# A hybrid attention layer in fp32 on one core: stationary operands of 64 rows become operands of 128 rows

## The chip, the cores and the metric

One of the eight cores of a Trainium2 chip runs the kernel. The metric is the device time of one execution in microseconds (us), from the first to the last instruction. TensorE multiplies matrices, VectorE (DVE), ScalarE (ACT) and GpSimd (POOL) work elementwise, and SyncE (SP) issues most of the DMAs. Before a TensorE matmul its stationary operand has to be loaded into the array by an instruction of its own, LDWEIGHTS, which the profile lists as an engine PEld. The matmul then streams the moving operand through the array. A stationary operand of 128 rows by 128 columns fills the array; its rows are the axis that is summed over.

## The reference, cut to what matters

One layer of a decoder on 1024 tokens of width 1024, all in fp32. Three attentions run side by side on projections of the same normalised input; their gated sum is projected, and an MLP with a hidden width of 4096 follows. The edits touch the first attention (4 heads with two score maps each) and the compressed part of the third (8 heads in 2 groups, 63 compressed keys and values per group).

```python
# first attention: q, k [token, head, c, 64], v [token, head, 128]
s = jnp.einsum('bqhcd,bkhcd->cbhqk', qi, k).astype(jnp.float32) * scale + bias
p = jax.nn.softmax(jnp.where(mask, s, NEG_INF), axis=-1)
w = p[0] - lam * p[1]
return jnp.einsum('bhqk,bkhe->bqhe', w.astype(v.dtype), v)
...
# third attention, compressed part: kc, vc [block, group, 64]
s = jnp.einsum('bsgrd,bcgd->bgrsc', qg, kc).astype(jnp.float32) * scale
p_cmp = jnp.where(cmask, jax.nn.softmax(jnp.where(cmask, s, NEG_INF), axis=-1), 0.0)
o_cmp = jnp.einsum('bgrsc,bcgd->bsgrd', p_cmp.astype(vc.dtype), vc).reshape(B, S, H, D)
```

## The kernel before

**Numbers in two parts.** An fp32 value x is held as a high part (x rounded to the fp32r type that TensorE reads) and a low part x - high. `split` makes both: ScalarE copies the high part (L90), VectorE or GpSimd subtracts for the low part (L91). A dense product then takes three matmuls in `mm3`, high*high, high*low and low*high, at lines L118 to L120.

**Stages.** The program runs: normalisation and transposes of x while the first head's projection is made (the pool `p0` holds the buffers of that), the vectors of the relative position bias (`bias_vectors`), the compressor of the third attention's keys and values (pool `cp`), the first attention (stage A, `items_a`, four heads), the second (`items_b`), the third (stage C, `items_c`, two groups of four heads), then the merge of the branches and the MLP. TensorE's program order is the order in which the code is written; the order on the other engines comes from a scheduler. In the attentions `mix` weaves two streams into TensorE's order: the fine one (logits, transposes of probabilities, value products) and a dense one (the next head's projection in `project`, or the gates), by paces written in the code.

**Stage A.** For each head `project` computes 8 token tiles of q, k, v (384 columns). `vec` in `project_a` normalises them and lays q and k out in `tm`, 128 columns a block, and `to_state` turns the blocks over by TensorE transposes (L552), in groups of up to four, and copies each group to the state tile `st` (four blocks at a time on VectorE, L558, the fifth alone on ScalarE, L556). For map c the q block holds the high and the low part of q on 128 rows (64 each). The block `2 + c` of the state holds the high part of k twice, on both halves of the rows. The fifth block holds the low parts of k once for both maps: c = 0 on rows 0 to 63, c = 1 on rows 64 to 127. `logits` (L705) makes a score map of 64 to 512 columns in PSUM from two matmuls, with q as the stationary operand:

```python
n["logits"].append([(st[:, c * S:c * S + S], st[:, (2 + c) * S:(3 + c) * S]),
                    (st[half, c * S:c * S + S], st[half, 4 * S:5 * S])])
```

The first is a stationary operand of 128 rows (high and low q, against high k), the second one of 64 rows (high q alone, against low k). Between the row steps of an item stand projection matmuls with operands of 128 rows. VectorE finds each row's minimum (L719 and L729), ScalarE takes the exponential (L737) into `p` and so frees the logits' buffer (three buffers, `sc`), TensorE transposes `p` (L753), the result is split into `ph` and `pl`, and the value products follow two steps later.

**Stage C.** Each item (a head and 256 queries, 32 in all) begins with the compressed part: the logits of 64 compressed keys, masked, their exponentials `pc` (128 queries x 64), two transposes of `pc` into a tile of 64 rows, its split, and two value products with `vct` as the stationary operand (L895 with the high part of the probabilities, L896 with the low part). `vct` has 64 rows, the compressed blocks, and 128 columns, the high and the low part of the values. It writes the accumulator `ac`, of which there is one buffer, freed when the last item's output has been read (L902).

**Queues around it.** The loads of weights, of x and of the bias vectors' inputs (`rb`, `oh`, `mk`, lines L370 to L374) go through SP's queue, where an instruction that waits holds all behind it. The matmuls of `bias_vectors` (L378) stand between the first head's projection and the compressor's projection, whose weights are the eight loads of `wk`.

Of the kernel before, what the change touches and what calls it, by code (L numbers as in the profile page):

```python
# [11 lines left out]
F32 = mybir.dt.float32  # L12
# [5 lines left out]
P = 128  # L18
# [57 lines left out]
class Kernel:  # L76
# [97 lines left out]
    def run(self):  # L174
# [24 lines left out]
        self.st_n, self.tm_n = 7 * S, 768  # L199
# [7 lines left out]
        with tc.tile_pool(name="p0", side="right", **kw) as p0:  # L207
# [36 lines left out]
            self.bias_vectors(p0)  # L244
        with tc.tile_pool(name="cp", side="right", **kw) as cp:

            w1 = self.states[0].tile([P, 7, 4, 256], F32, name="w1", tag="st", bufs=1)
            for i in range(7):
                nc.sync.dma_start(w1[:, i], a["w1"][i // 4, :, (i % 4) * 4:(i % 4) * 4 + 4, :])
            z = self.compress_inputs(cp)  # L250
            self.spread_bias(0)
            self.mm = mm2
            self.mix(self.compress(cp, z, w1), self.gates(GATES[0]), PACE[5])
# [30 lines left out]
        nc.sync.dma_start(self.cmask, a["c_cmask"])  # L284
        for g in range(2):
# [41 lines left out]
    def constants(self, tmp):  # L327
# [36 lines left out]
        self.vct = c.tile([64, 2, P], F32R, name="vct")  # L364

    def bias_vectors(self, pool):
# [8 lines left out]
        bv = pool.tile([20, 2, 384], F32, name="bv")  # L375
        for i in range(2):
            ps = self.mm()
            nc.tensor.matmul(ps[0:20, 0:384], rb, oh[:, i, :], start=True, stop=True)  # L378
            nc.vector.tensor_tensor(bv[:, i, :], ps[0:20, 0:384], mk[:, i, :], op=ALU.add)
        self.bs = self.dram.tile([20, 2, 384], F32, name="bs")  # L380
        nc.sync.dma_start(self.bs, bv)
# [39 lines left out]
    def compress(self, cp, z, w1):  # L421
# [37 lines left out]
        for kv in range(2):  # L459
# [22 lines left out]
            else:  # L482
# [3 lines left out]
                self.split(self.vct[:, :, 0:64], self.vct[:, :, 64:128], vr)  # L486
# [81 lines left out]
    def project_a(self, h):  # L568
# [4 lines left out]
        n = dict(st=st, v=st[:, 5 * S:7 * S].rearrange("p (t x e) -> p t x e", x=2, e=P), logits=[])  # L573
        for c in range(2):
            half = slice(64 * c, 64 * c + 64)
            n["logits"].append([(st[:, c * S:c * S + S], st[:, (2 + c) * S:(3 + c) * S]),
                                (st[half, c * S:c * S + S], st[half, 4 * S:5 * S])])
        gain = self.gk[:, 0:1, :].to_broadcast([P, 2, HD])

        def vec(t, raw):  # L580
# [8 lines left out]
            kl = tm[:, 512:640].rearrange("p (c d) -> p c d", d=HD)  # L589
            nc.vector.tensor_tensor(kl, y[:, 2:4, :], kd[:, :, 0, :].bitcast(F32), op=ALU.subtract)  # L590
            return tm

        return self.project(self.a["wa"][h], 384, vec, (st, [i * S for i in range(5)])), n
# [364 lines left out]
    def items_c(self, g, sta):  # L958
        nc, at = self.nc, self.at
        bias4 = self.bias  # L960
        for r in range(4):
            for qb in range(4):
# [104 lines left out]
                def pv_c(blk=blk, hv=hv):  # L1067
                    ph, pl = blk["p"]
                    return hv(self.vct[:, g, :], ph[0:64, 0:256], pl[0:64, 0:256], True, False)
# [15 lines left out]
    def compressed(self, mem, ps, t):  # L1085

        nc = self.nc
        p = mem["c"] = self.at.tile([P, 64], F32, name="pc", tag="pc", bufs=4)
        m, l = mem["m"], mem["l"]
        nc.vector.tensor_tensor_reduce(ps, ps, self.cmask[:, t, :], 1.0, 3e38, ALU.add, ALU.min, m[:, 0, 0:1])  # L1090
        self.expo(p, ps, m[:, 0, 0:1], l[:, 0, 0:1])
# [490 lines left out]
```

## Time and profile before

| what | value |
|---|---|
| median of 3 executions | 2076.6 us (2073.64 to 2076.71) |
| span of the profiled execution | 2073.6 us |
| mean granted TensorE clock | 0.983 of full speed |
| TensorE matmuls | 1950.6 us busy (94%), 9806 instructions |
| TensorE weight loads | 1615.6 us (78%) |
| VectorE | 1420.5 us (69%) |
| ScalarE | 1019.3 us (49%) |
| GpSimd | 948.4 us (46%) |
| DMA | 219.47 MB, mean 106 GB/s |

The profiled execution has no time of its own beside its span: the span, 2073.6 us, equals the fastest of the three times, 2073.64, so nothing lies around it that the time counts.

A matmul's row gives the columns of its tile, the stationary operand as rows*columns and the shape of the moving operand; `64*128 64x512` is 64 rows by 128 columns against 512 columns. Matmuls are pipelined and overlap: the busy time of one is longer than the distance to the next one's start. So this text takes distances from start to start for what a matmul costs.

### The profile page before, as it was taken

Reading aid. Unit: us, or ns where it says so; the run is one execution under the profiler, and the core shown is the slowest. Engines: PE = TensorE matmul, PEld = TensorE weight load, DVE = VectorE, ACT = ScalarE, POOL = GpSimd, SP = SyncE. Lnnn points to the kernel's source line nnn. Section 1 sums busy time; section 2 is a strip of 40 time slices with the busy share of each in tenths; the row PEclk is TensorE's granted clock in tenths of the full one; section 3 lists DMA queues with packets and bytes.
Section 4 is the critical chain, followed back from the end, with each engine's and each line's share of the span. In section 5 each row is a group of like instructions: output and inputs, shape, how many; then the busy total and the mean of one; then the engine's idle time right before and its main releaser. Section 6 shows DMA issues by size and latency. Waiting matters only on the chain. (4 is left out here: it accounts for less than half of the span.)

```text
span 2073.6 us, 30616 instructions
## 1 busy us (share of the span) xinstructions
PE 1950.6 (94%) x9806; PEld 1615.6 (78%) x9806; DVE 1420.5 (69%) x3231; ACT 1019.3 (49%) x2626; POOL 948.4 (46%) x1137
## 2 busy tenths in 40 slices
PE   7999998998899999999999899999899998999998
PEld 7777777788688788787888677787688886888876
DVE  6757677788838767648676745657755444889898
ACT  5456555566636555536555533325445544434331
POOL 4555345354252212152221327217444444789784
PEclk9999999999999999999999899999999999999998
DMA  6131012011201111202142556425544346345343
GB/s 216 50 102 52 3 55 58 14 50 37 85 24 64 54 53 50 71 30 93 61 151 64 168 180 208 153 89 159 173 163 155 138 143 249 121 158 168 122 142 112
DMA packets 122557, 219.47 MB, mean 106 GB/s; under 512 B 14420, under 2 KB 35412, under 8 KB 122396
## 3 DMA queue, kind: packets, MB, share of 16 engines
q1 hardware_dynamic: 120812, 211.75, 31.3%
q10 hardware_dynamic: 1584, 5.77, 0.8%
q8 instruction: 77, 1.26, 0.3%
q14 instruction: 84, 0.69, 0.1%
HBM read 156.59 MB, written 64.81 MB: 107 GB/s over the span
## 5 line engine op out<-in xcount | busy, mean ns | idle before, releaser
L91 POOL TENSOR_TENSOR wl<-wr,wh 128x512 fp32r<-128x512 f32 (+3 forms) x246 | 326.1, 1332 | 282.1 <-ACT wh L90 236.8
L90 ACT ACTIVATE wh<-wr 128x512 fp32r<-128x512 f32 (+3 forms) x258 | 150.4, 591 | 182.3 <-PE mm L119 122.5
L705 PE MATMUL sc<-st 128*128 128x256 f32 (+5 forms) x736 | 201.6, 356 | 15.4 <-ACT p L737 15.0
L90 ACT ACTIVATE ph<-tr 128x384 fp32r<-128x384 f32 (+3 forms) x280 | 138.3, 496 | 118.0 <-PE tr L753 97.1
L91 DVE TENSOR_TENSOR pl<-tr,ph 128x384 fp32r<-128x384 f32 (+3 forms) x280 | 155.3, 558 | 45.7 <-ACT ph L90 42.4
L750 POOL MEMSET ph<- 128x128 f32 x152 | 34.7, 228 | 301.2 <-PE ac L895 256.6
L705 PEld LDWEIGHTS sc<-st 128*128 128x128 f32 x736 | 126.3, 192 | 55.7 <-ACT p L737 23.4
L118 PE MATMUL mm<-hh,wh 128*128 128x512 f32 x384 | 160.0, 417 | 0.0
L120 PE MATMUL mm<-hh,wl 128*128 128x512 f32 x384 | 152.5, 397 | 0.0
L119 PE MATMUL mm<-hl,wh 128*128 128x512 f32 x384 | 152.4, 397 | 0.0
L119 PE MATMUL mm<-wl,wh 128*128 128x512 f32 x352 | 140.4, 399 | 9.4 <-POOL wl L91 9.4
L118 PE MATMUL mm<-wh 128*128 128x512 f32 x352 | 140.5, 399 | 8.3 <-DVE x L1464 5.4
L753 PE MATMUL tr<-ident,p 128*128 128x128 f32 x792 | 132.3, 280 | 15.4 <-ACT o L883 7.9
L90 ACT ACTIVATE wh<-u 128x512 fp32r<-128x512 f32 x162 | 93.1, 620 | 107.8 <-PE mm L119 28.0
L120 PE MATMUL mm<-wh,wl 128*128 128x512 f32 x352 | 139.7, 397 | 0.0
L737 ACT ACTIVATE p<-sc,mc 128x256 f32<-128x256 f32 (+5 forms) x200 | 106.8, 538 | 51.0 <-DVE mc L729 48.9
L895 PE MATMUL ac<-ph,st 128*128 128x256 f32 x392 | 111.4, 302 | 17.2 <-DVE ob L902 11.3
L91 POOL TENSOR_TENSOR wl<-s,wh 128x512 fp32r<-128x512 f32 x64 | 87.8, 1379 | 82.8 <-ACT wh L90 82.8
L118 PE MATMUL mm<-wh,hh 128*128 128x384 f32 (+1 forms) x320 | 124.6, 389 | 0.0
L91 DVE TENSOR_TENSOR wl<-u,wh 128x512 fp32r<-128x512 f32 x98 | 110.4, 1128 | 4.1 <-ACT wh L90 4.1
L896 PE MATMUL ac<-pl,st 128*128 128x256 f32 x392 | 106.6, 293 | 5.8 <-DVE pl L91 5.2
L753 PEld LDWEIGHTS tr<-ident,p 128*128 128x128 f32 x792 | 92.0, 142 | 24.8 <-ACT o L883 10.5
(309 smaller groups left out, 5759.6 us busy)
## 6 DMA issues: line engine op xcount, KB each, us to landing
ud<-u SPq DMA_DIRECT2D x112, 256.0 KB, 2.1
u<-ud SPq DMA_DIRECT2D x98, 256.0 KB, 3.3
wr<-wu SPq DMA_DIRECT2D x76, 256.0 KB, 2.8
wr<-wd SPq DMA_DIRECT2D x64, 256.0 KB, 2.9
gd<-go SPq DMA_DIRECT2D x48, 256.0 KB, 2.0
g<-gd SPq DMA_DIRECT2D x48, 256.0 KB, 3.1
wr<-wg SPq DMA_DIRECT2D x40, 256.0 KB, 2.6
wr<-wbr SPq DMA_DIRECT2D x40, 256.0 KB, 3.0
```

The lines of the kernel that those rows point to most:

```text
L90: nc.scalar.activation(hi, src, AF.Copy)
L91: (eng or nc.vector).tensor_tensor(lo, src, hi.bitcast(F32), op=ALU.subtract)
L118: mm(out, lh, rh, start=first, stop=False, skip_group_check=more)
L119: mm(out, lh, rl, start=False, stop=False, skip_group_check=more)
L120: mm(out, ll, rh, start=False, stop=last, skip_group_check=more)
L705: self.nc.tensor.matmul(ps[:, off:off + k1 - k0], q[:, t * P:(t + 1) * P], k[:, k0:k1], start=i == 0, stop=i == 1)
L737: self.nc.scalar.activation(p, ps, AF.Exp, bias=m, scale=-1.0, accum_out=l)
L750: nc.gpsimd.memset(ph[0:rows, o:o + P].bitcast(F32), 0.0)
L753: nc.tensor.transpose(pt[0:rows, o:o + P], src, self.ident)
L895: nc.tensor.matmul(ac, v, ph, start=first, stop=False)
L896: nc.tensor.matmul(ac, v, pl, start=False, stop=last)
```

## The change

**Keys.** In stage A the low parts of the keys stand twice, on both halves of the rows, for each map a block of its own. The second matmul of each score map then has the same stationary operand as the first, all 128 rows of q, and adds the product of the low parts of q and k, which was left out before. The state tile grows from 7 to 8 blocks of 1024 columns, `tm` is used to its full width of 768, the subtraction for the low part covers 256 columns instead of 128, and `to_state` turns six blocks over for each token tile instead of five.

**Compressed values.** `vct` gets 128 rows, of which the lower 64 are zero. The probabilities `pc` are four lasting tiles of 128 columns, of which the right 64 are set to zero once; their transposes then have 128 rows.

**Bias vectors.** Their inputs are allocated in the pool `cp` instead of `p0`, and the sum is written over `mk`.

```diff
-        self.st_n, self.tm_n = 7 * S, 768
+        self.st_n, self.tm_n = 8 * S, 768
...
-            self.bias_vectors(p0)
         with tc.tile_pool(name="cp", side="right", **kw) as cp:
+            self.bias_vectors(cp)
...
+        self.pcs = [self.at.tile([P, P], F32, name=f"pc{i}") for i in range(4)]
+        for x in self.pcs:
+            nc.gpsimd.memset(x[:, 64:P], 0.0)
...
-        self.vct = c.tile([64, 2, P], F32R, name="vct")
+        self.vct = c.tile([P, 2, P], F32R, name="vct")
+        nc.gpsimd.memset(self.vct[64:P].bitcast(F32), 0.0)
...
-            nc.vector.tensor_tensor(bv[:, i, :], ps[0:20, 0:384], mk[:, i, :], op=ALU.add)
+            nc.vector.tensor_tensor(mk[:, i, :], ps[0:20, 0:384], mk[:, i, :], op=ALU.add)
...
-                self.split(self.vct[:, :, 0:64], self.vct[:, :, 64:128], vr)
+                self.split(self.vct[0:64, :, 0:64], self.vct[0:64, :, 64:128], vr)
...
-        n = dict(st=st, v=st[:, 5 * S:7 * S].rearrange("p (t x e) -> p t x e", x=2, e=P), logits=[])
+        n = dict(st=st, v=st[:, 6 * S:8 * S].rearrange("p (t x e) -> p t x e", x=2, e=P), logits=[])
         for c in range(2):
-            half = slice(64 * c, 64 * c + 64)
-            n["logits"].append([(st[:, c * S:c * S + S], st[:, (2 + c) * S:(3 + c) * S]),
-                                (st[half, c * S:c * S + S], st[half, 4 * S:5 * S])])
+            q = st[:, c * S:c * S + S]
+            n["logits"].append([(q, st[:, (2 + c + x) * S:(3 + c + x) * S]) for x in (0, 2)])
...
-            kl = tm[:, 512:640].rearrange("p (c d) -> p c d", d=HD)
-            nc.vector.tensor_tensor(kl, y[:, 2:4, :], kd[:, :, 0, :].bitcast(F32), op=ALU.subtract)
+            kl = tm[:, 512:768].rearrange("p (c x d) -> p c x d", x=2, d=HD)
+            nc.vector.tensor_tensor(kl, y[:, 2:4, :].unsqueeze(2).to_broadcast([P, 2, 2, HD]), kd.bitcast(F32),
+                                    op=ALU.subtract)
...
-        return self.project(self.a["wa"][h], 384, vec, (st, [i * S for i in range(5)])), n
+        return self.project(self.a["wa"][h], 384, vec, (st, [i * S for i in range(6)])), n
...
-                    return hv(self.vct[:, g, :], ph[0:64, 0:256], pl[0:64, 0:256], True, False)
+                    return hv(self.vct[:, g, :], ph[:, 0:256], pl[:, 0:256], True, False)
...
-        p = mem["c"] = self.at.tile([P, 64], F32, name="pc", tag="pc", bufs=4)
+        p = mem["c"] = self.pcs[0]
+        self.pcs.append(self.pcs.pop(0))
...
-        self.expo(p, ps, m[:, 0, 0:1], l[:, 0, 0:1])
+        self.expo(p[:, 0:64], ps, m[:, 0, 0:1], l[:, 0, 0:1])
```

TensorE's order is otherwise the same; the two matmuls of a score map were one row of the order before and are now. In stage A, where the projection of the next head is woven in (`tm` holds the laid out q and k, `st` the state, `ac` the output), it read before:

```order
L118 MATMUL mm<-wh,hh 128x384
L119 MATMUL mm<-wl,hh 128x384
L120 MATMUL mm<-wh,hl 128x384
L552 MATMUL tr<-identr,tm 128x128
L118 MATMUL ac<-ph,st 128x256
```

and now:

```order
L118 MATMUL mm<-wh,hh 128x384
L119 MATMUL mm<-wl,hh 128x384
L120 MATMUL mm<-wh,hl 128x384
L555 MATMUL tr<-identr,tm 128x128 x2
L118 MATMUL ac<-ph,st 128x256
```

One transpose more stands at each place where the fifth block was turned over alone.

On SP's queue at the start of the program (`x` are the tiles of the input, `w` the compressor's first weights, `wr<-wk` the compressor's projection weights, `rb`, `oh` and `mk` the bias vectors' inputs) it read before:

```order
L214 DMA x<-x 128x1024 x2
L370 DMA rb<-rel_bias 32x20
L214 DMA x<-x 128x1024
L372 DMA oh<-c_oh 32x768
L374 DMA mk<-c_mk 20x768
L249 DMA w_773<-w 128x1024 x7
L214 DMA x<-x 128x1024
L100 DMA wr<-wk 128x256 x8
```

and now:

```order
L214 DMA x<-x 128x1024 x2
L249 DMA w_778<-w 128x1024
L214 DMA x<-x 128x1024
L249 DMA w_778<-w 128x1024 x6
L100 DMA wr<-wk 128x256 x3
L214 DMA x<-x 128x1024
L100 DMA wr<-wk 128x256
L374 DMA rb<-rel_bias 32x20
L376 DMA oh<-c_oh 32x768
L378 DMA mk<-c_mk 20x768
L100 DMA wr<-wk 128x256 x4
```

The three loads of the bias vectors' inputs stand behind the first four loads of `wk`, and the last load of `x` stands behind three of them.

More of the change, by code (lines that the diff above doesn't have):

```diff
@@ L374, in bias_vectors @@
         nc.sync.dma_start(mk, a["c_mk"])
-        bv = pool.tile([20, 2, 384], F32, name="bv")
         for i in range(2):
@@ L378, in bias_vectors @@
             nc.tensor.matmul(ps[0:20, 0:384], rb, oh[:, i, :], start=True, stop=True)
-            nc.vector.tensor_tensor(bv[:, i, :], ps[0:20, 0:384], mk[:, i, :], op=ALU.add)
+            nc.vector.tensor_tensor(mk[:, i, :], ps[0:20, 0:384], mk[:, i, :], op=ALU.add)
         self.bs = self.dram.tile([20, 2, 384], F32, name="bs")
-        nc.sync.dma_start(self.bs, bv)
+        nc.sync.dma_start(self.bs, mk)
         self.bd = [self.dram.tile([4, P, 384], F32, name=f"bd{i}") for i in range(5)]
```

## The prediction

> **What bounds the kernel now.** I read the engine times by window first, then who waits for whom inside the two stages that the edits touch, then the timeline of TensorE around single instructions. The columns of the first view are the window, its length, and the busy time (with the number of instructions) of TensorE matmuls, TensorE weight loads, VectorE, ScalarE and GpSimd; then the granted TensorE clock, the DMA share and GB/s.
>
> ```profile
> 128.00:448.00 320.00, 298.61 (x1672) 246.10 (x1670) 228.03 (x663) 179.36 (x597) 148.90 (x230) 1.00 0.14 41
> 621.00:1217.00 596.00, 565.08 (x3113) 474.42 (x3112) 414.00 (x1293) 329.09 (x933) 156.50 (x281) 0.98 0.24 76
> 480.00:550.00 70.00, 60.91 (x387) 54.22 (x388) 61.94 (x218) 48.16 (x164) 28.10 (x83) 0.98 0.23 63
> 550.00:600.00 50.00, 44.97 (x219) 36.53 (x218) 25.49 (x79) 20.00 (x61) 20.36 (x46) 0.92 0.19 53
> ```
>
> The first row is the first attention (stage A): TensorE idles 21.4 of 320 us (6.7%), VectorE is busy 71%. The second is the third attention (stage C): TensorE idles 5.2%, VectorE is busy 69%. (The last two lie in the second attention and just behind its end.) Stages A and C are TensorE-bound, and the waits of A agree: in the list of waits for stage A (engine and line, for whom, us in total, times, longest) VectorE's row minima (L719) stand waiting for logits.
>
> ```profile
> DVE m L719 <- PE sc L705: 14.3, 30, 1.0
> ```
>
> But a busy TensorE isn't a TensorE at its peak. The timeline (start, us, engine, line, operation, tiles, stationary rows*columns, moving operand, idle before) shows two pairs of logits matmuls among projection matmuls, first the matmuls, then the weight loads:
>
> ```profile
> 163.53 0.49 PE L753 MATMUL tr<-ident,p 128*128 128x128 f32 x3
> 163.77 0.91 PE L705 MATMUL sc<-st 128*128 128x512 f32 x2
> 164.62 0.44 PE L118 MATMUL mm<-wh,hh 128*128 128x384 f32 x1
> 164.90 0.34 PE L119 MATMUL mm<-wl,hh 128*128 128x384 f32 x1
> 165.07 0.34 PE L120 MATMUL mm<-wh,hl 128*128 128x384 f32 x1
> 165.24 0.70 PE L705 MATMUL sc<-st 128*128 128x384 f32 x2
> 165.88 0.44 PE L118 MATMUL mm<-wh,hh 128*128 128x384 f32 x1
> 166.16 0.34 PE L119 MATMUL mm<-wl,hh 128*128 128x384 f32 x1
> ```
>
> ```profile
> 164.18 0.18 PEld L705 LDWEIGHTS sc<-st 64*128 64x128 f32 x1 [0.25 <-issue]
> 164.61 0.19 PEld L118 LDWEIGHTS mm<-wh,hh 128*128 128x128 f32 x1 [0.25 <-issue]
> 164.72 0.19 PEld L119 LDWEIGHTS mm<-wl,hh 128*128 128x128 f32 x1
> 165.51 0.18 PEld L705 LDWEIGHTS sc<-st 64*128 64x128 f32 x1 [0.25 <-issue]
> 165.88 0.19 PEld L118 LDWEIGHTS mm<-wh,hh 128*128 128x128 f32 x1 [0.18 <-issue]
> ```
>
> The load for L119 at 164.72 starts while the matmul of 164.62 still runs: its cost is hidden. The load of a 64-row operand doesn't start early, and neither does the 128-row load behind it: each stands idle 0.18 to 0.25 us with nothing that it waits for. Between 128-row operands a 384-wide matmul follows the last after 0.17 us (164.90 to 165.07 to 165.24).
>
> **The change, part by part: what goes.** The second pair takes from 165.24 to 166.16, when L119 runs again after one L118: 0.92 us for three 384-wide matmuls, against 3 x 0.175 = 0.53 undisturbed. It loses 0.39 us. The first takes 1.13 us (163.77 to 164.90), against 0.23 + 0.23 + 0.175 (0.23 for 512 columns, from the rows at 648 below): 0.49 lost. The view by form (count, busy, mean ns, idle before) gives the number of such pairs and their exposed time:
>
> ```profile
> L705 PEld LDWEIGHTS sc<-st 64*128 64x128 f32 x96 | 17.5, 183 | 22.4 <-issue 21.1
> L118 PEld LDWEIGHTS mm<-wh,hh 128*128 128x128 f32 x320 | 60.0, 188 | 18.1 <-issue 13.7 <-ACT raw L514 0.5
> ```
>
> 96 pairs, with 21.1 + 13.7 = 34.8 us of weight-load idleness that nothing explains, 0.36 each. I take 0.39 for each: 96 x 0.39 = **37.4 us** less TensorE time in stage A (bounds: 34.8 from the idle, 47 from the longer pair).
>
> By the Trainium skill (TensorE: Matmul & The Clock Gate, Part 3, "What overlaps and what doesn't") a weight load overlaps a running matmul only when the row groups differ; then a 128-row load behind a 128-row matmul would be exposed too, and widening would gain nothing. The load at 164.72 contradicts it here.
>
> In stage C the compressed values are the stationary operand of two 64-row matmuls per item, 32 items:
>
> ```profile
> 648.34 0.39 PE L119 MATMUL mm<-hl,wh 128*128 128x512 f32 x1
> 648.57 0.40 PE L120 MATMUL mm<-hh,wl 128*128 128x512 f32 x1
> 648.90 0.39 PE L895 MATMUL ac<-ph,vct 64*128 64x256 f32 x1
> 649.13 0.28 PE L896 MATMUL ac<-pl,vct 64*128 64x256 f32 x1
> 649.34 0.55 PE L753 MATMUL tr<-ident,p 128*128 128x128 f32 x3
> 649.64 0.48 PE L118 MATMUL mm<-hh,wh 128*128 128x512 f32 x1
> ```
>
> ```profile
> 423.13 0.28 PE L120 MATMUL ac<-ph,st 128*128 128x256 f32 x1
> 423.25 0.28 PE L118 MATMUL ac<-ph,st 128*128 128x256 f32 x1
> ```
>
> ```profile
> PE ac L895 <- DVE ob L902: 8.1, 9, 1.2
> ```
>
> From 648.57 to 649.64 pass 1.07 us. With 0.23 for the 512-wide one (648.34 to 648.57), 0.12 for each 256-wide one (423.13 to 423.25) and 0.24 for three transposes (163.53 to 163.77) it would be 0.71: 0.36 lost, 11.5 us in 32 items. In 9 of them L895 waits for the freed accumulator anyway, which hides the 0.10 ahead of it: **10.6 us** remain (bounds 8.3, should the first 0.10 go nowhere, and 11.5).
>
> The Trainium skill (TensorEngine Tiling, "Key Properties") has a change of tiling mode drain TensorE. That fits the borders, but L895 and L896 have the same mode and 0.23 us between them; by the rule alone that 0.11 would stay, 3.5 us less gain. The form is the same, so I go by the row.
>
> **What is added.** One transpose per token tile and head, 32: L552 at x1 takes 0.06 us of TensorE.
>
> ```profile
> 162.71 0.22 PE L552 MATMUL tr<-identr,tm 128*128 128x128 f32 x1
> 162.77 0.33 PE L118 MATMUL ac<-ph,st 128*128 128x256 f32 x1
> ```
>
> That is 1.4 us in stage A (24) and 0.5 before it (8, while head 0 is projected). VectorE's subtraction for the low part of the keys doubles to 256 columns, and ScalarE's copy to the state goes from 128 to 256:
>
> ```profile
> L590 DVE TENSOR_TENSOR tm<-y,tm 128x128 fp32r<-128x128 f32 x32 | 11.2, 350 | 2.1 <-ACT tm L588 1.7
> ...
> L530 DVE TENSOR_TENSOR y<-raw,ssq 128x256 f32<-128x256 f32 x32 | 15.6, 486 | 7.2 <-POOL ssq L126 7.2
> L556 ACT ACTIVATE st<-tr 128x128 fp32r<-128x128 f32 x32 | 8.6, 267 | 21.3 <-PE tr L552 21.3
> L556 ACT ACTIVATE st<-tr 128x256 fp32r<-128x256 f32 x32 | 12.1, 378 | 22.7 <-PE tr L552 22.6
> ```
>
> 24 x 0.136 = 3.3 us of VectorE and 24 x 0.11 = 2.7 us of ScalarE in stage A, beside engines that idle 29% and 44% there; without that cover at most 6.0 us. The transposes of the compressed probabilities get 128 columns instead of 64; the moving operand, 128 columns, stays, and so should their pace (below zero nothing speaks for it; above, 64 x 0.06 us = 3.8 at most, were each to cost one more transpose like L552's). One memset of 64x256 and four of 128x64 come on GpSimd, the first at the program's start and the others ahead of stage C's first L527:
>
> ```profile
> 6.25 0.56 POOL L126 TENSOR_TENSOR ss<-ss,nhalf 128x1 f32<-128x1 f32 x1 [4.95 <-DVE ss L125]
> ...
> 578.41 0.83 POOL L527 TENSOR_TENSOR y<-raw 128x384 f32<-128x384 f32 x1 [8.60 <-ACT raw L514]
> ```
>
> GpSimd idles 4.95 and 8.60 us there, so I cost them at nothing; without that cover they would be some 2 us, an estimate of five pieces at half this 128x384 row's 0.83.
>
> The bias vectors move. Their three loads go on SP's queue from ahead of the compressor weights to between the fourth and fifth load of wk, and their tiles now take memory that the normalisation of x leaves.
>
> ```profile
> L135 DVE SCALAR_TENSOR_TENSOR xn<-x,ss,g x8: 1284/1548/1926, 7.8 to 45.1; 128x1024 f32<-128x1024 f32 x8
> ...
> 23.87 37.59 SPq L100 DMA_DIRECT2D wr<-wk  x8
> ...
> 61.97 1.46 PE L378 MATMUL sc<-oh,rb 32*20 32x384 f32 x4
> ```
>
> The last reader of that memory starts at 45.1 and lasts some 1.6 us, the matmuls that need the vectors come at 62.0, and the eight wk loads are spread over 37.6 us because they wait for freed buffers. The load of x that now stands behind three of them serves the last row of that kind, at 45.1. Queued behind the new wait are only the last four of these, which can't go before their buffers are free near 59. I cost it at nothing; should the three loads come out only with the fifth wk, they would hold TensorE by about 1 us.
>
> **From TensorE time to the span.** A faster TensorE meets the softmax chain more often. The two stages above show how idleness grows: at 71% VectorE (stage A) TensorE idles 6.7%, at 88.5% (the row 480 to 550, 61.94 of 70) it idles 13.0%. In stage A the work becomes 298.6 - 37.4 + 1.4 = 262.6 us; VectorE has 231.3 us, about 80% of 290, and between the two rows that is 9.9% idle: 262.6 / 0.901 = 291.4, **28.6 us** less than 320. What is late next are the exponentials that free logits buffers and the splits of transposed probabilities. In stage C 565.1 - 10.6 = 554.5 us at 5.6% idle gives 587.4, **8.6 us** less. With 0.5 us added before: 36.7 us, 2073.6 - 36.7 = 2036.9 for an execution like the profiled one. That one was the fastest of the three; the median, 2076.6, is 3.0 higher, so I add 2 for the median: **2039 us**.
>
> **The rivals.**
> - *The softmax chain takes most of it.* If TensorE waits out half of each saving in both stages, and the 6.0 us added on VectorE and ScalarE lie on the path: 18.7 + 5.3 - 1.9 - 6.0 = 16 us, 2058, for the median 2060. For it: waits for the chain already exist; against it: VectorE itself waits 14.3 us for logits in the row of L719. Chance 0.09.
> - *All of it stays, and more.* 37.4 - 1.4 + 11.5 - 0.5 = 47 us, 2027, which the range still holds; with 0.49 a pair 2017. Below the range: 0.04.
> - *It does not do what it says.* If the load behind a 128-row operand of another tile is exposed all the same, nothing goes and 1.9 us of transposes come: 2075.5, for the median 2077.5. The overlapped loads speak against it: 0.03. (The Trainium skill's rule of Part 3, above, would give this.)
> - *Slower: the granted clock drops in stage A.* It is 1.00 there now; from 550 to 600, where TensorE idles 10%, it is 0.92. Idling 9.9% could bring that on, and the 291.4 us would become 291.4 / clock. At 0.92 that is 317 and the kernel still gains some 11 us; from 0.89 down (328 us, stage C's gain eaten too) it loses; at 0.85, 343 us and 2088. Against it: from 480 to 550 TensorE idles 13% at 0.98. 0.04.
>
> **How the numbers follow.** The forecast has 0.80. Its range is 2025 (everything kept, fast execution) to 2055 (half of stage A's 37.4 kept, the 6.0 of added work on the path, C's 8.6 kept, 0.5 and 1.4 added: 2054); it leaves out most of the first rival and the other three. About 0.2% (4 us) is what a measurement of this kernel can tell from no change. Faster: 0.80 + 0.09 + 0.04 = 0.93; same 0.03; slower 0.04.
>
> **What would show it.** Right: no weight load with 64 rows in stages A and C; a 384-wide pair of logits and the next L118 in about 0.53 us; stage A's matmuls through some 29 us sooner after its start; 0.12 us from L895 with vct to L896. The softmax rival shows as TensorE idle above 12% in stage A, the clock rival in the clock of the windows, the bias loads as a gap ahead of L378. I am wrong if the 64-row loads go and the L118 behind them still idles.

## The result, and the profile after

Measured together, the changed kernel takes 2050.5 us (median of 4 executions, 2048.11 to 2055.95), the kernel before 2075.1 us (4 executions, 2072.13 to 2076.71): the ratio is **0.988, with a 95% interval of 0.9861 to 0.99**. The forecast was 2039 us in a range of 2025 to 2055: the sign and the range held, and a third of the expected gain is missing.

The profiled execution took 2048.11 us, with a span of 2046.0. First its engine times by window for stage A (first attention) and stage C (third attention), with each stage's own bounds. The columns are those of the prediction's first view (window, length, busy time and instructions of TensorE, weight loads, VectorE, ScalarE and GpSimd; granted clock, DMA share, GB/s). Before:

```profile
128.10:442.80 314.70, 293.31 (x1636) 240.97 (x1635) 223.38 (x648) 176.82 (x589) 146.73 (x225) 1.00 0.15 42
621.10:1216.60 595.50, 564.58 (x3111) 473.98 (x3109) 413.90 (x1293) 328.99 (x932) 156.50 (x281) 0.98 0.24 76
```

After:

```profile
128.70:422.90 294.20, 261.06 (x1660) 242.29 (x1659) 226.52 (x648) 179.63 (x588) 146.82 (x225) 1.00 0.16 45
603.30:1188.60 585.30, 551.32 (x3111) 470.20 (x3109) 413.46 (x1293) 329.10 (x932) 156.41 (x281) 0.99 0.25 77
```

Stage A went from 314.7 to 294.2 us, 20.5 less, where 28.6 were forecast. TensorE's busy time fell by 32.3 us, but its idle time (length less busy) grew from 21.4 to 33.1, 11.8 more. Stage C lost 10.2 us, where 8.6 were forecast, but its clock was 0.98 before and 0.99 after, so a part of that is the clock's (more below). The other stages differ by 3 us at most: start +0.6, second attention +2.1, merge +2.8, the projections behind it -2.4 together. The sum is the 27.6 us between the spans.

The timeline of TensorE after (start, us, engine, line, operation, tiles, stationary rows*columns, moving operand, idle before) has the 384-wide pair of logits at the same place in the program, now L708 and 128 rows throughout. First matmuls, then weight loads:

```profile
161.41 0.51 PE L708 MATMUL sc<-st 128*128 128x384 f32 x2
161.76 0.34 PE L118 MATMUL mm<-wh,hh 128*128 128x384 f32 x1
161.94 0.34 PE L119 MATMUL mm<-wl,hh 128*128 128x384 f32 x1
```

```profile
161.24 0.36 PEld L708 LDWEIGHTS sc<-st 128*128 128x128 f32 x2
161.59 0.19 PEld L118 LDWEIGHTS mm<-wh,hh 128*128 128x128 f32 x1
161.77 0.19 PEld L119 LDWEIGHTS mm<-wl,hh 128*128 128x128 f32 x1
```

From 161.41 to 161.94 pass 0.53 us, where it was 0.92 before. The load for L118 starts at 161.59, while the pair still runs. The groups of weight loads by form (whole program; count, busy, mean ns, idle before) say the same of all of them:

```profile
L708 PEld LDWEIGHTS sc<-st 128*128 128x128 f32 x736 | 121.6, 191 | 47.6 <-ACT p L740 38.7
L118 PEld LDWEIGHTS mm<-wh,hh 128*128 128x128 f32 x320 | 60.4, 189 | 1.7
```

The 96 loads with 64 rows are gone, with their 21.1 us of unexplained idleness, and L118's 13.7 us as well. In stage C the products with the compressed values (now L898, L899) follow each other and the next transposes in 0.12 us:

```profile
630.73 0.40 PE L120 MATMUL mm<-hh,wl 128*128 128x512 f32 x1
630.97 0.28 PE L898 MATMUL ac<-ph,vct 128*128 128x256 f32 x1
631.09 0.29 PE L899 MATMUL ac<-pl,vct 128*128 128x256 f32 x1
631.21 0.49 PE L756 MATMUL tr<-ident,p 128*128 128x128 f32 x3
631.45 0.48 PE L118 MATMUL mm<-hh,wh 128*128 128x512 f32 x1
```

That is 0.72 us from 630.73 to 631.45 where it was 1.07. So the price of a single place was right; what was short is how much of it reached the end of stage A. TensorE's waits in stage A (who waits, for what, us in total, times, longest) show where it went. Before:

```profile
PE tr L753 <- ACT o L883: 7.2, 10, 0.9
PE tr L753 <- DVE pl L91: 4.1, 5, 1.1
PE tr L753 <- DVE st L558: 2.8, 4, 0.8
PE tr L881 <- DVE st L558: 1.7, 3, 1.0
PE sc L705 <- ACT p L737: 1.7, 3, 1.1
```

After:

```profile
PE sc L708 <- ACT p L740: 10.1, 12, 2.2
PE tr L756 <- ACT o L886: 7.0, 10, 0.9
PE tr L756 <- DVE pl L91: 4.9, 5, 1.2
PE tr L756 <- DVE st L561: 3.6, 4, 1.2
PE tr L884 <- DVE st L561: 3.3, 3, 1.2
```

One wait is new in size: the logits matmul waits for the exponential that frees one of the three `sc` buffers, 12 times and 10.1 us instead of 3 times and 1.7. That is 8.4 of the 11.8 us. (The longest, 2.2 us at 134.5, is the first wait of the stage and was there before with 1.1 us.)

### The profile page after: what moved, and what is told of

It reads as the page before. It is cut to its first block, busy times and chain, and to the rows that moved or that the text cites. A ratio compares the mean times of both kernels' runs of the same rounds, so it can differ in the third digit from the quotient of the medians.

```text
span 2046.0 us, 30701 instructions
## 1 busy us (share of the span) xinstructions
PE 1903.3 (93%) x9838; PEld 1612.2 (79%) x9838; DVE 1426.5 (70%) x3231; ACT 1023.1 (50%) x2626; POOL 949.1 (46%) x1142
## 5 line engine op out<-in xcount | busy, mean ns | idle before, releaser
L708 PE MATMUL sc<-st 128*128 128x256 f32 (+5 forms) x736 | 182.6, 342 | 26.1 <-ACT p L740 25.5
L118 PE MATMUL mm<-hh,wh 128*128 128x512 f32 x384 | 159.8, 416 | 0.0
L708 PEld LDWEIGHTS sc<-st 128*128 128x128 f32 x736 | 121.6, 191 | 47.6 <-ACT p L740 38.7
L119 PE MATMUL mm<-hl,wh 128*128 128x512 f32 x384 | 152.1, 396 | 0.0
L119 PE MATMUL mm<-wl,wh 128*128 128x512 f32 x352 | 139.4, 396 | 9.3 <-POOL wl L91 9.3
L118 PE MATMUL mm<-wh 128*128 128x512 f32 x352 | 139.9, 398 | 8.2 <-DVE x L1468 5.3
L898 PE MATMUL ac<-ph,st 128*128 128x256 f32 x392 | 109.5, 297 | 19.9 <-DVE ob L905 11.4
L118 PE MATMUL mm<-wh,hh 128*128 128x384 f32 (+1 forms) x320 | 115.5, 361 | 0.0
L899 PE MATMUL ac<-pl,st 128*128 128x256 f32 x392 | 105.6, 290 | 6.0 <-DVE pl L91 5.3
L91 POOL TENSOR_TENSOR wl<-u,wh 128x512 fp32r<-128x512 f32 x64 | 97.9, 1544 | 26.2 <-ACT wh L90 26.2
```

Of the source, the lines that this page charges most:

```text
L91: (eng or nc.vector).tensor_tensor(lo, src, hi.bitcast(F32), op=ALU.subtract)
L118: mm(out, lh, rh, start=first, stop=False, skip_group_check=more)
L119: mm(out, lh, rl, start=False, stop=False, skip_group_check=more)
L708: self.nc.tensor.matmul(ps[:, off:off + k1 - k0], q[:, t * P:(t + 1) * P], k[:, k0:k1], start=i == 0, stop=i == 1)
L898: nc.tensor.matmul(ac, v, ph, start=first, stop=False)
L899: nc.tensor.matmul(ac, v, pl, start=False, stop=last)
```

## The experiments

The theory: a 64-row operand cost what the timeline showed, and TensorE, now faster, runs into the softmax chain, which gives back part of stage A. The main rivals: the work that the change adds (more transposes, wider copies and subtractions) causes the waits; or the move of the bias vectors has a share. Four kernels take the change apart. All four, as the later ones, are compared with the kernel before on the same chip; it had medians of 2073.6 to 2074.6 us there.

### The keys alone

The changed kernel, the move of the bias vectors included, with before's 64-row `vct` and `pc`.

```diff
-        self.vct = c.tile([P, 2, P], F32R, name="vct")
+        self.vct = c.tile([64, 2, P], F32R, name="vct")
...
-                    return hv(self.vct[:, g, :], ph[:, 0:256], pl[:, 0:256], True, False)
+                    return hv(self.vct[:, g, :], ph[0:64, 0:256], pl[0:64, 0:256], True, False)
```

> The keys' half of the change alone (low parts of the keys twice, six blocks turned over, the bias vectors' move that its memory needs); the compressed values stay at 64 rows. If each 64-row operand costs its own exposed load and nothing else ties the parts together, stage A shortens by the 20.5 us of the whole change and stage C not at all: about 18 to 20 us less than before. If the two parts hinder each other (a faster A shifts what C collides with), the sum of this run and of the values alone differs from the whole change by more than 4 us.

Measured: 2059.6 us, ratio 0.9928 (0.9908 to 0.9947). That is 14.9 us by the medians, less than the 18 to 20 expected; with the run below the two parts add up to 21.1 us, 3.5 from the 24.6 of the whole change, so they don't hinder each other by the mark of 4 us. Stage A behaves as in the changed kernel (idle 33.7 us, 10.9 of them for the exponential). In the profiles it is 22.8 us shorter than with the bias move alone (the section after the next; clocks 0.99 and 0.98), while the rest of the program is 7.1 us longer; that wasn't traced further.

### The compressed values alone

The kernel before with the padded `vct` and `pc`, so the other half of the same diff.

> The compressed values' half alone (vct and the probabilities padded with zeros to 128 rows); keys and bias vectors as before. By the exposed loads: 0.36 us in each of 32 items, less what waits for the accumulator hide: 8 to 10 us less than before, all of it in stage C. If only a change of mode costs (128 to 64 rows and back), L895 to L896 stays at 0.23 us here too and the gain is 6 us.

Measured: 2068.4 us, ratio 0.9965 (0.995 to 0.9979). By the medians that is 6.1 us, the rival's number and not the 8 to 10 expected (the interval allows 4.4 to 10.4). But the rival's mechanism fails: the two products stand 0.12 us apart (median of 32 items), where it would have left 0.23. Stage A stays near before's idle time (23.2 us); its waits for the exponential stay small, 2.5 us.

### The move of the bias vectors alone

```diff
-            self.bias_vectors(p0)
+            self.bias_vectors(cp)
```

> Only the bias vectors' inputs move to the later pool and the sum is written over the mask. Theory: nothing, within 0.1% (2 us) of before, the loads land long before the matmuls at 62 us. Rival: the move costs part of what the whole change lacks against the forecast, 2 us or more, seen as a gap ahead of the bias matmuls or of the compressor's projection.

Measured: 2074.6 us, ratio 0.9997 (0.998 to 1.0014): nothing. The keys' run holds this move already; with the compressed values' run it multiplies to 0.9928 x 0.9965 = 0.989, inside the whole change's interval. Stage C in the window view, first this kernel, then the one with the compressed values alone, then one with padded values from further below (the last section of the experiments):

```profile
627.20:1218.90 591.70, 560.19 (x3110) 470.19 (x3108) 413.26 (x1293) 328.94 (x932) 156.59 (x281) 0.99 0.24 76
```

```profile
626.40:1210.00 583.60, 550.07 (x3110) 469.19 (x3108) 413.03 (x1293) 329.27 (x932) 156.85 (x281) 0.99 0.24 77
```

```profile
606.30:1192.00 585.70, 552.47 (x3110) 471.04 (x3108) 412.33 (x1293) 328.80 (x932) 156.43 (x281) 0.99 0.25 77
```

All three say 0.99, yet the clocks aren't equal: by the traces' clock records the first and the third spent 13.7 us of the stage at half clock, the second 6.8. At equal clocks, first against third, the padding takes 7.7 us of TensorE's busy time and 6.0 us of the stage; first against second it looks like 10.1 and 8.1. The forecast was 10.6 and 8.6. Free of the clock is a count by items: from the matmul ahead of the two products to the one behind the transposes, less the wait for the accumulator, all 32 items together take 8.8 us less here and 8.6 in the changed kernel. An item without that wait saves 0.34 us, as in the timelines shown; the nine that wait save 0.15.

### The added work without the full rows

The changed kernel does all its extra transposes, copies and subtractions, but its matmuls read 64 rows again, of the keys and of the compressed values.

```diff
-            n["logits"].append([(q, st[:, (2 + c + x) * S:(3 + c + x) * S]) for x in (0, 2)])
+            half = slice(64 * c, 64 * c + 64)
+            n["logits"].append([(q, st[:, (2 + c) * S:(3 + c) * S]),
+                                (st[half, c * S:c * S + S], st[half, (4 + c) * S:(5 + c) * S])])
...
-                    return hv(self.vct[:, g, :], ph[:, 0:256], pl[:, 0:256], True, False)
+                    return hv(self.vct[0:64, g, :], ph[0:64, 0:256], pl[0:64, 0:256], True, False)
```

> All work that the change adds (double low parts, sixth transposes, 256-wide copies, padded tiles) is done, but the second matmul of each score map and the value products read only 64 rows again, so the 64-row loads are back. My theory (added work is nearly free, the shortfall of stage A is waiting that a faster TensorE meets): 1 to 4 us above before, TensorE's waits in stage A about 11 us as before. Rival (the added work on VectorE and ScalarE lies on the path and eats the missing 8 us of stage A): 8 us or more above before, and waits in stage A well above 11 us.

Measured: 2085.3 us, ratio 1.0051 (1.0031 to 1.007), slower than before, and 10.7 us by the medians, where I had expected 1 to 4. So the gain comes from the rows alone, and the added work isn't free. Stage A with the bias move alone, then with the added work, at the same clock:

```profile
128.30:449.00 320.70, 297.90 (x1636) 244.80 (x1635) 223.06 (x648) 176.63 (x589) 146.06 (x225) 0.98 0.15 42
```

```profile
129.10:454.50 325.40, 299.39 (x1660) 246.29 (x1659) 227.41 (x648) 179.16 (x588) 146.57 (x225) 0.98 0.14 41
```

The stage is 4.7 us longer: 1.5 us of TensorE, as forecast for 24 transposes, and 3.2 us of idle time (22.8 to 26.0). VectorE has 4.4 us and ScalarE 2.5 us more. The whole kernel loses more than that. Of the 12.6 us between the two spans, 3.8 lie in stage C, where this kernel reads 64 rows like before; it had before's length and clock there, 595.5 us at 0.98, against 591.7 at 0.99. The other 4.1 us are spread over the start (0.8), the second attention (1.3) and what follows stage C (2.0). That rest wasn't traced further.

### Full rows without the added work

Before's five blocks (and its place of the bias vectors), with all 128 rows of q against the one block of low keys. The second product then also has low q times the low part of the other map's keys, a term that doesn't belong to the result. The compressed values are padded.

```diff
-            n["logits"].append([(q, st[:, (2 + c + x) * S:(3 + c + x) * S]) for x in (0, 2)])
+            n["logits"].append([(q, st[:, (2 + c) * S:(3 + c) * S]), (q, st[:, 4 * S:5 * S])])
```

> The state of before, with one block of low keys (map 0 on rows 0 to 63, map 1 on rows 64 to 127), but both matmuls of a score map read all 128 rows of it and of q; vct padded as in the change. The second product then adds, beside the wanted high q times low k, the low part of q times the low keys of the other map, which the reference does not have (a term of the size of the low*low product that before leaves out). No sixth transpose, no doubled subtraction, no wider copy. If the added work is what the change gives back (5 us of stage A by the run with added work alone, 10 by its median), this is 5 to 10 us faster than the change, 2040 to 2046. If the shortfall is waiting that a faster TensorE meets whatever the added work, it is within 3 us of the change, 2048 to 2053, with TensorE idle in stage A still about 33 us.

Measured: 2048.8 us, ratio 0.9872 (0.9852 to 0.9892), not to be told from the changed kernel. TensorE's wait in stage A is the same in sum without the extra work:

```profile
PE sc L708 <- ACT p L740: 10.2, 12, 3.9
```

This and the run before separate the two causes, though not cleanly. The added work alone, with a slow TensorE, makes 3.2 us of idle time; with the fast TensorE and without that work the stage still idles 33.2 us, against 33.1 and 33.7 in two profiles of the changed kernel. But the sums hide a difference. The first wait of the stage differs from run to run: 2.2 and 2.9 us in those two profiles, 3.9 here. The other eleven add up to 7.9 us in both profiles of the changed kernel and to 6.3 here, and 1.3 of these 1.6 us lie at the two longest, which take 1.0 us here and 1.6 to 1.7 there. So most of the wait comes from the faster TensorE, and a smaller part from the added work. (The length of the stage, 298.4 us, doesn't show that part: it spent 13.7 us at half clock, by the trace's clock records, against none and 6.8 in the two profiles of the changed kernel.)

### The low parts of the keys on GpSimd

The doubled subtraction (L592) leaves VectorE for GpSimd.

```diff
-            nc.vector.tensor_tensor(kl, y[:, 2:4, :].unsqueeze(2).to_broadcast([P, 2, 2, HD]), kd.bitcast(F32),
+            nc.gpsimd.tensor_tensor(kl, y[:, 2:4, :].unsqueeze(2).to_broadcast([P, 2, 2, HD]), kd.bitcast(F32),
```

> The change, with the doubled subtraction of the keys' low parts on GpSimd instead of VectorE. If VectorE's share of the added work (256 instead of 128 columns) sits on the path of the logits' buffers, stage A gains 3 to 6 us and the waits of the logits for the exponentials fall from 10 us towards 5. If it is the transposes and copies, or only the speed of TensorE, nothing moves by more than 2 us; GpSimd's longer subtraction (about 0.8 us at 256 columns) may even cost 1 to 3 us.

Measured: 2052.0 us, ratio 0.989 (0.9872 to 0.9908), the same as the changed kernel. VectorE has 4.4 us less in stage A, GpSimd 17 more, and the wait is unmoved at 10.0 us (13 times). That doesn't clear VectorE, for beside GpSimd's subtraction two of its instructions ran slower, just ahead of the minimum (L732) that the exponential at one of the two longest waits needs:

```profile
231.37 1.48 POOL L592 TENSOR_TENSOR tm<-y,tm 128x256 fp32r<-128x256 f32 x2
231.52 0.73 DVE L91 TENSOR_TENSOR tm<-y,tm 128x128 fp32r<-128x128 f32 x1
232.18 0.69 DVE L725 TENSOR_TENSOR m<-m 128x1 f32<-128x1 f32 x1
```

At the same place of the changed kernel they last 0.28 and 0.15 us. The 0.99 us more are about what the two subtractions took on VectorE (0.44 and 0.42), and this wait fell only from 1.68 to 1.54 us. So the run doesn't tell what the wait would be with a VectorE that has less to do; the run above, with 4.3 us less on VectorE and nothing more on GpSimd, tells it better.

### Compressed values on 96 rows

The products with `vct` read 96 of the 128 rows; the other 32 are zeros, so the result is the same.

```diff
-                    return hv(self.vct[:, g, :], ph[:, 0:256], pl[:, 0:256], True, False)
+                    return hv(self.vct[0:96, g, :], ph[0:96, 0:256], pl[0:96, 0:256], True, False)
```

> The change, with the value products of the compressed part reading 96 rows (the 64 real ones and 32 zero rows). If any operand of fewer than 128 rows has an exposed load, L898 to L899 is again 0.23 us and stage C loses its 8 to 10 us. If only operands of one half of the rows do, it stays at 0.12 us and the time is the change's.

Measured: 2054.5 us, ratio 0.9905 (0.9886 to 0.9924), which overlaps the changed kernel's interval. The timeline of TensorE:

```profile
635.28 0.28 PE L898 MATMUL ac<-ph,vct 96*128 96x256 f32 x1
635.40 0.28 PE L899 MATMUL ac<-pl,vct 96*128 96x256 f32 x1
635.52 0.49 PE L756 MATMUL tr<-ident,p 128*128 128x128 f32 x3
```

0.12 us each, as with 128 rows, where 64 rows took 0.23 and 0.21. So the price isn't one for any operand of fewer than 128 rows: 64 rows have it and 96 haven't. Nothing in between was run.

### The pace of the projection, up and down

In stage A the dense stream (the next head's projection) is woven in by a pace: the more of it, the more cover a row step has, and the sooner it runs out. If the waits come from a pace that is wrong for the faster TensorE, another pace should take them away. First the changed kernel with 1.75 instead of 1.6:

```diff
-PACE = (1.6, 1.4144, 1.156, 1.392, 1.45, 1.7)
+PACE = (1.75, 1.4144, 1.156, 1.392, 1.45, 1.7)
```

> The change, with the weave of stage A at pace 1.75 instead of 1.6: more projection matmuls between two row steps, fewer left for a head's end. If the new waits come from row steps that arrive sooner than the exponentials free the logits' buffers, these waits (10 us) fall and stage A gains 2 to 5 us, or they come back as waits at the head's end. If the pace is not what decides, within 2 us of the change.

Measured: 2073.1 us, ratio 0.9992 (0.9979 to 1.0004): the change's gain is lost. Then 1.5, in the kernel with full rows and no added work:

```diff
-PACE = (1.6, 1.4144, 1.156, 1.392, 1.45, 1.7)
+PACE = (1.5, 1.4144, 1.156, 1.392, 1.45, 1.7)
```

> The form of e5 (all 128 rows of q against before's five blocks, values padded), and the first attention's pace, which sets how many projection matmuls go ahead of a row step by the softmax work that VectorE still has to do, from 1.6 to 1.5. Pace 1.75 made stage A wait more (TensorE idle 43.6 us instead of 33.1), because the projection runs out ahead of the head's last row steps. If the waiting is set by how the projection is spread, 1.5 should lower the idle time in stage A from e5's 33.2 us to below 30 and the time from 2048.8 to about 2044. If the pace was already at its best for the faster TensorE, or less projection ahead of a row step exposes the softmax chain more, idle stays at 33 or grows to above 36, and the time is 2048 to 2054.

Measured: 2061.4 us, ratio 0.9939 (0.9925 to 0.9953), a miss as well. The execution profiled took 2072.2 us, the other five 2060.4 to 2063.3, so the idle time of its stage A may be above the usual. Stage A in the window view, at 1.75 and then at 1.5:

```profile
127.50:447.70 320.20, 276.56 (x1660) 258.50 (x1659) 227.79 (x647) 180.11 (x588) 144.55 (x226) 0.94 0.15 42
```

```profile
127.30:442.90 315.60, 268.62 (x1636) 249.30 (x1635) 217.92 (x648) 178.68 (x589) 142.97 (x225) 0.97 0.15 42
```

TensorE idles 43.6 and 47.0 us, more than at 1.6 on both sides, and its granted clock is 0.94 and 0.97. At 1.75 its busy time is 15.5 us above the changed kernel's 261.1, which fits that clock (an estimate: 6% of 320 us are 19 us at most). So 1.6 is the best of the three paces, each of the others was tried in one of the two forms alone, and neither took the waiting away.

### The order of the row minima on VectorE

What holds the exponential at the two longest new waits (0.27 and 0.28 us before the change) is seen in the timeline of the changed kernel at 228 to 235 us (head 1; head 2 has the same 72 us later):

```profile
230.91 0.63 PE L708 MATMUL sc<-st 128*128 128x512 f32 x2
...
231.39 0.42 DVE L592 TENSOR_TENSOR tm<-y,tm 128x256 fp32r<-128x256 f32 x1
...
231.73 0.68 DVE L722 TENSOR_REDUCE m<-sc 128x1 f32<-128x512 f32 x1
...
232.33 0.48 DVE L732 CUSTOM_DVE_ANT_0 sc<-sc,bias,m 128x256 f32<-128x256 f32 x1
...
232.90 0.69 ACT L740 ACTIVATE p<-sc,m 128x512 f32<-128x512 f32 x1 [0.90 <-DVE m L732]
...
233.73 0.62 PE L708 MATMUL sc<-st 128*128 128x384 f32 x2 [1.68 <-ACT p L740]
```

Read it from the bottom: TensorE waits 1.68 us for ScalarE's exponential of 232.90, ScalarE waited 0.90 us for the minimum L732 of 232.33, and on VectorE's queue stood in front of that a subtraction of the projection (L592) and the first minimum of the other map (L722, 0.68 us), which nobody needed yet. The experiment issues that minimum behind L732.

```diff
-                return self.logits(ps, 0, t, sta["logits"][c], 0, mem["n0"]), self.far_min(m, 1, ps[:, 0:mem["n0"]])
+                cost = self.logits(ps, 0, t, sta["logits"][c], 0, mem["n0"])
+                if c == 1:
+                    with self.tc.issue_after(self.near_ins):
+                        return cost, self.far_min(m, 1, ps[:, 0:mem["n0"]])
+                return cost, self.far_min(m, 1, ps[:, 0:mem["n0"]])
```

> The change, but on VectorE the first minimum of map 1 is issued behind the second minimum of map 0, where the scheduler had put it in front. In the changed kernel the two places where it stands in front (at 232 and at 305 us, heads 1 and 2) are those where TensorE then waits 1.68 and 1.63 us for the exponential that frees a logits buffer. If VectorE's order makes these waits, stage A's waits of the logits matmul for the exponential fall from 10.1 us to about 7, both long waits become under 0.8 us, idle in stage A falls from 33.1 to about 31, and the time goes from 2050.5 to about 2048. If the exponentials are late for another cause (ScalarE's own queue, or the projection's vectors ahead of them), the waits stay at 10 us and the time at 2050 to 2053.

Measured: 2049.2 us, ratio 0.9884 (0.9867 to 0.9901), the same as the changed kernel. In the trace the two waits went from 1.68 and 1.63 to 1.07 and 1.04 us, and the idle time from 33.1 to 31.3:

```profile
PE sc L708 <- ACT p L741: 9.0, 12, 2.2
```

The mechanism is shown, since each wait shrank by 0.6 us, nearly the 0.68 that the minimum lasts; but it is a third of these two waits and 1.2 us in all, so the 7 us and the waits under 0.8 that I expected were missed. In the kernel without the added work these two waits are 1.00 us each, and there the scheduler had put L732 in front of L722 by itself, with a shorter subtraction (0.29 us) ahead; with the subtraction on GpSimd it did so too. So at these two places it is the doubled subtraction on VectorE that comes with the turned order, and this is where the added work costs its 1.3 us. What is left isn't one late instruction, but a chain of minimum, exponential and three buffers that is late at 12 places.

### Both small gains together, and the change once more

The kernel with full rows and no added work (the diff of one section) and the order of minima (the diff of another); beside it the changed kernel again on the same chip.

> The form of e5 (all 128 rows of q against before's five blocks) with the order of minima of e10. If the second copy of the low keys costs 3 to 5 us in stage A as e4 and e5 suggest, and the order of minima gains another 1 to 2 us, the time is 2044 to 2047, below the changed kernel's by more than the interval when both run on one chip. If the added work lies beside other work and the order is worth nothing, it is 2049 to 2051, the same as the changed kernel.

> The changed kernel itself once more, with more runs, on the chip of e12: 2048 to 2052 and a ratio to before of 0.987 to 0.989 if the first measurement holds. It is the yardstick for e12: a difference under 2 us between them is none.

Measured: 2047.0 us (4 executions, 2045.58 to 2048.96; ratio 0.987, 0.9852 to 0.9889) and 2049.3 us (4 executions, 2048.30 to 2051.59; ratio 0.9884, 0.9862 to 0.9905). The second repeats the first measurement. The 2.2 us between them are no more than 0.1%, the two ranges touch and the intervals overlap: whether the added work and the order still cost 2 us is not settled, and no version here beats the change by what can be measured. The two gains were one, too: without the added work the minima stand in the good order already, and the two waits are 0.99 and 1.01 us here where they were 1.00 without the edit. Stage A doesn't settle it either (first the combination, then the change):

```profile
128.20:427.30 299.10, 267.40 (x1636) 248.11 (x1635) 223.03 (x648) 177.33 (x588) 145.93 (x225) 0.97 0.16 45
```

```profile
127.90:425.90 298.00, 264.33 (x1660) 245.41 (x1659) 225.76 (x648) 179.69 (x588) 147.32 (x226) 0.99 0.16 45
```

The combination idles 2.0 us less (31.7 against 33.7), but it ran at a lower clock in this execution: 20.5 us of the stage at half clock against 6.8, by the traces' clock records.

## Why the prediction was right, and where it fell short

**0.39 us a pair: right.** Pair by pair in program order, the time from the pair's start to that of the second matmul behind it (L119, as in the prediction's 0.92 us) fell by a median of 0.39 us, at 256, 384 and 512 columns alike; so the 0.49 of the longer pair wasn't lost. All 96 pairs together give 36.7 us, for the 37.4 of the prediction. The Trainium skill (TensorE: Matmul & The Clock Gate, Part 3, "What overlaps and what doesn't") lets a load overlap only when row groups differ. The load at 161.59, with 128 rows behind 128 rows, overlaps and the rows decide against the rule, as the prediction held.

**The compressed values: the mechanism right, the size somewhat high.** 8.6 to 8.8 us of TensorE by items and 6.0 of the stage at equal clocks, for 10.6 and 8.6. The sum had the wait for the accumulator hide 0.10 us in nine items; it hides 0.19. The 0.11 us between the two products went too. The drain at a change of mode that the Trainium skill states (TensorEngine Tiling, "Key Properties") would have left it; the row of before was the better guide. The Trainium skill's list of modes (TensorEngine Tiling, "Tiling Modes") has 128, 64 and 32 rows and none of 96; no run shows under which of them such an operand falls, only that its 0.12 us is that of 128 rows.

**The transposes: right.** 1.5 us of TensorE for the forecast 1.4 in stage A; and those of `pc` keep their pace at 109 ns each, with 128 rows as with 64.

**The added elementwise work beside others: only partly.** I costed it at nothing, with a bound of 6.0. With TensorE slow it made 3.2 us of idle time in stage A. With TensorE fast, leaving it out changes the idle time by 0.5 us at most and the waits for the exponential, but for the first, by 1.6. The medians without it are some 2 us lower, which is not clear of the noise. Why the kernel with the work and without the rows lost 10.7 us stays open.

**The move of the bias vectors: right**, at 0.9997. L381, which needs them, starts at 61.86, where it was 61.97:

```profile
61.86 1.46 PE L381 MATMUL sc<-oh,rb 32*20 32x384 f32 x4
```

**From TensorE time to the span: this term was mis-sized.** The prediction drew a line between two rows, 6.7% idle at 71% VectorE and 13.0% at 88.5%, and took 9.9%. Stage A now idles 11.3% (33.1 of 294.2) with VectorE at 77%, where the line has 8.8%. The forecast for the stage was 36.0 us less work and 7.4 more idle time, 28.6 in all. Measured were 32.3 us less busy time and 11.8 more idle time, 20.5 in all. So of the missing 8.1 us, 4.4 are idle time and 3.7 are busy time that didn't go. Of these 3.7, 0.7 are the pairs (36.7 for 37.4). Some 2 are an estimate from the two traces: TensorE stops to wait 39 times instead of 29, and the matmul ahead of a stop counts about 0.2 us more, since none overlaps its end. (The prediction's window for stage A, 320 us, held 5.2 us of the second attention; by the same line on the stage's own 314.7 us the forecast is 29.1, which changes nothing.)

The line used VectorE's busy share as the measure of how late the softmax chain is. It isn't a good one: in the kernel without the added work VectorE has 4.3 us less to do, and the stage idles the same 33.2 us. What the traces suggest in its place is latency, from a pair of logits through minimum and exponential to the freed buffer, against the time in which TensorE works off what stands between. The change shortened the latter, and its added work lengthened the former at two places; there a minimum issued earlier shortened the waits by nearly as much. For the other places that is argued and not shown. My first rival has the chain absorb half of the saving; the forecast had 21% (7.4 of 36.0), and stage A lost 37% (11.8 of 32.3), between the two. The rival's own sign, idle above 12%, wasn't reached, and stage C kept 6.0 of 7.7.

**The granted clock: hardly a loss here.** Stage A of the changed kernel was at 1.00 and, in the second profile, 0.99. The paces that made TensorE idle 13.6 and 14.9% had 0.94 and 0.97, so a loss as in the rival does occur. But the share of idle time doesn't order the clocks: 0.97 also came at 10.6%, in the last combination, and 0.98 at 7.1%, with the bias vectors moved alone.

**Span and time: wrong, and covered by chance.** I took the span for the execution's own time. The profiled execution of the changed kernel took 2048.11 us at a span of 2046.0, so 2.1 us lie around it, and in every other execution with both numbers it is 1.7 to 2.1. That the span of the kernel before equals one of its three times is a coincidence. The 2 us that I added for another reason stood for them.

## What to carry to other kernels

A small operand in the middle of large ones can cost more than its own work: look for weight loads that stand idle and wait for nothing, and measure from start to start what the neighbours lose. To know what such a gain is worth, don't take an engine's busy share as its slack: follow the next wait in the trace (here three buffers that an exponential frees) and count its latency, since a TensorE with 11% less to do in a stage meets it at 12 places instead of 3. When work is added to feed a full operand, price it both ways, in a kernel that has the work and not the gain and in one that has the gain and not the work: here the first said 10.7 us and the second about 2.

## What the hardware showed beside that

TensorE's clock drops to half for stretches of 3.4 us, one or several in a row, and in other places in other runs. Stage A of the kernel with only the bias vectors moved, and then of the kernel before at the first of these times:

```profile
137.20:140.60 3.40, 3.40 (x10) 2.20 (x8) 1.79 (x6) 1.04 (x4) 1.03 (x2) 0.50 0.00 0
140.60:144.00 3.40, 3.40 (x10) 3.07 (x11) 2.11 (x10) 1.37 (x5) 1.15 (x2) 0.50 0.00 0
359.00:362.40 3.40, 3.40 (x11) 3.27 (x11) 2.46 (x9) 2.22 (x9) 0.24 (x1) 0.50 0.11 39
```

```profile
137.20:140.60 3.40, 3.40 (x18) 2.88 (x18) 2.65 (x12) 1.55 (x5) 2.17 (x3) 1.00 0.00 0
```

In the first of them the engine has 10 matmuls where it had 18. The two kernels have the same work in stage A, yet it takes 320.7 and 314.7 us. The first spends 10.2 us of the stage at half clock, in these three stretches, and the second none; that is 5.1 us of work, most of the 6.0 between them. It is a quarter of what the change saves there, so profiles of two kernels should be compared at equal clocks, and two digits of the mean clock aren't enough for it, as stage C showed. The Trainium skill (TensorE: Matmul & The Clock Gate, Part 1, "What's actually happening") has a gate that judges TensorE's activity in windows of about 3.4 us and halves the rate; length and rate agree with these rows. What set it off in one run and not in another isn't shown.
